# Attention scores of 64-row heads: one head on each half of TensorE's rows, instead of zero-padded queries on all 128 rows

## The chip, the core and the metric

The kernel runs on one core of one Trainium2 chip. The metric is the device time of one execution in microseconds (us). Matrix products run on TensorE (in the profile: PE for the matmul, PEld for the load of its stationary operand), elementwise work on VectorE (DVE), ScalarE (ACT) and GpSimd (POOL); transfers are issued from SyncE (SP). TensorE multiplies a stationary operand (up to 128 rows by 128 columns) with a moving one (the same rows, up to 512 columns) and adds into a bank of the accumulator memory (128 partitions by 512 fp32), of which there are eight.

## What is computed

Two layers of an encoder trunk on one sequence of 256 tokens, width 1024, in fp32. Each layer is a half-step feed-forward block, a mixer, a second half-step feed-forward block and a gated input embedding. The mixer's first half is neighbourhood attention with 8 heads of 64 channels, and only its scores are touched here:

```python
D_MODEL, SEQ, DEPTH, D_FF = 1024, 256, 2, 2816
NA_HEADS, NA_HEAD_DIM = 8, 64
...
    for i in range(DEPTH):
        x = x + 0.5 * swiglu(rmsnorm(x, g_ffa[i]), w_ffa_gate[i], w_ffa_up[i], w_ffa_down[i])
        u = rmsnorm(x, g_mix[i]) @ w_in[i]
        q, k, v, hy = jnp.split(u, [NA_WIDTH, 2 * NA_WIDTH, 3 * NA_WIDTH], axis=-1)
        y_na = neighbourhood_attention(q, k, v, na_rpb[i])   # scores, bias, mask, softmax, values
        ...                                                  # Hyena long convolution -> y_hy
        x = x + concat([_rms(y_na), _rms(y_hy)]) * g_out[i] @ w_out[i]
        x = x + 0.5 * swiglu(rmsnorm(x, g_ffb[i]), w_ffb_gate[i], w_ffb_up[i], w_ffb_down[i])
        x = x + jax.nn.sigmoid(rmsnorm(x, g_ple[i]) @ w_ple_gate[i]) * (p[i] @ w_ple_proj[i])
    return rmsnorm(x, g_final)
```

The kernel computes the scores of a head densely, all 256 queries against all 256 keys. Scaling, bias and mask (-1e30 outside the neighbourhood) come in one pass afterwards, and then the softmax.

## The kernel before

**Precision.** Every fp32 operand is split into a high part, rounded to the TensorE format fp32r, and a low part, the remainder. A product is the sum of three matmuls: high by high, high by low, low by high. `mm3` (L169) issues these three in a row and then counts them with `paced`; `Wide.mm` and `Wide.flush` (L190, L197) do the same for 512-wide operands that hold high and low parts side by side. Splitting is an ACT copy to fp32r and a DVE subtraction. The weights are split in this way while the kernel runs (L285 on ACT, L288 on DVE, or on POOL for every third piece of the mixer).

**Order of the work.** The order on PE is the order of the program text, and that on ACT is the order in which the program emits its instructions. Work beside the matmuls (evictions, splits, softmax) is written as fibers, generators that advance one step at each tick. `paced` counts matmul groups and calls a tick after every third count (`TICK = 3`); a fiber's `finish` forces ticks until that fiber is done. The mixer follows a written list (L58):

```python
ORDER = "g0 q0 g1 s0 q1 g2 t0 s1 g3 q2 t1 p0 u0 q3 f0 s2 f1 p1 s3 t2 x0 x1 t3 i0 p2 p3 i1 i2 i3 a0 ..."
```

Here `q` projects the queries and keys of one pair of heads, `s` makes the scores of a pair, `t` transposes its probabilities, `p` multiplies them with the values; `g`, `x`, `u`, `f` and `i` belong to the convolution and `a` to the output projection. There are four pairs in a layer, so eight in the run.

**Queries and keys.** A pair's projection leaves one bank: queries in columns 0 to 255, keys in columns 256 to 511; rows (partitions) 0 to 63 belong to the first head of the pair and 64 to 127 to the second. `QK.go` (L727 to L744) multiplies with the row norms on DVE (L733) into `q`. Then ACT copies the keys' high part (L738) and the queries' high part, 64 rows at a time (L740), and DVE makes the low parts (L742, L744). The queries go into tiles `qh` and `ql` of 128 by 512 that POOL has set to zero (L728, L729): head 0 lies in rows 0 to 63 of columns 0 to 255, head 1 in rows 64 to 127 of columns 256 to 511, and the rest stays zero.

**Scores.** `Head.scores` (L754 to L761) takes a bank, and for each half `tt` of the queries calls `mm3` with 128 zero-padded query columns as the stationary operand and all 256 key columns as the moving one. All 128 rows take part; the zeros remove the other head. That is 6 matmuls of 128 rows for a head and 12 for a pair, first all of head 0, then all of head 1. Each head's softmax fiber (L763 to L781: two DVE passes, two ACT exponentials, a reciprocal, two ACT scalings) is spawned right after that head's matmuls. `turn` (L783, transposes on L788) needs the finished softmax, and its result is split on L797 and L799. `attend` (L812) is the product with the values; `head_norm` (L804) scales its result on L807 and squares it on L353.

**What else uses these engines near the scores.** `spectral` (L895 to L914) has DVE products on L902 and L903, a POOL combination on L908 and a split on L912 (ACT) and L914 (DVE).

Of the kernel before, what the change touches and what calls it, by code (L numbers as in the profile page):

```python
# [12 lines left out]
F32R = mybir.dt.float32r  # L13
# [5 lines left out]
P = 128  # L19
T = 256  # L20
# [60 lines left out]
def hybrid_trunk(ctx: ExitStack, tc: tile.TileContext, w, xT, pT, rpb, small, wf, zT, dft, idft, decay, out):  # L81
    nc = tc.nc
    V, S, G, PE = nc.vector, nc.scalar, nc.gpsimd, nc.tensor
# [15 lines left out]
    def nm(s):  # L99
        uid[0] += 1  # L100
        return f"{s}{uid[0]}"

    def bank():
        return psp.tile([P, 512], F32, tag="ps", name=nm("ps"))

    def t2(dt=F32, s="t"):
        return k2.tile([P, 512], dt, tag="k2", name=nm(s))

    def t1(dt=F32, s="s"):
        return k1.tile([P, T], dt, tag="k1", name=nm(s))  # L110

    def v2(ap):
        return ap.rearrange("p (a b) -> p a b", a=2)

    def f(ap):
        return ap.bitcast(F32)
# [31 lines left out]
    def spawn(gen, first=False):  # L148
        fb = Fiber(gen)
        Pace.live.insert(0 if first else len(Pace.live), fb)  # L150
        return fb

    def tick():
        if not Pace.inside:
            Pace.inside = True
            for fb in list(Pace.live[::-1] if NEWEST else Pace.live):
                fb.step()
            Pace.live[:] = [fb for fb in Pace.live if not fb.done]
            Pace.inside = False
# [5 lines left out]
    def rest(n):  # L165
        for _ in range(n):
            yield

    def mm3(o, lh, ll, rh, rl, start, stop):  # L169
        PE.matmul(o, lh, rh, start=start, stop=False)  # L170
        PE.matmul(o, lh, rl, start=False, stop=False)  # L171
        PE.matmul(o, ll, rh, start=False, stop=stop)  # L172
        paced(o.free_size() // T if hasattr(o, "free_size") else o.shape[-1] // T)

    def paced(n=1):
        if not Pace.inside:
            Pace.total += 1
            Pace.count += n
            while Pace.count >= TICK:
                Pace.count -= TICK  # L180
                tick()
# [114 lines left out]
    def half():  # L296

        n = Stream.used
        Stream.used += 1
        h, l, fb = Stream.ready.pop(n)  # L300
        fb.finish()
        refill(n - LAG)
        return h, l
# [150 lines left out]
    def rb2():  # L454
        return rb.unsqueeze(1).to_broadcast([P, 2, T])
# [213 lines left out]
    def mixer(i):  # L669
# [15 lines left out]
        for quarter in range(4):  # L685
            h, l = half()
            for k in range(2):
                c = 2 * quarter + k
# [30 lines left out]
        class QK:  # L719


            def __init__(self, b):
                self.kh, self.kl = t1(F32R), t1(F32R)
                self.qh, self.ql = t2(F32R), t2(F32R)
                self.fb = spawn(self.go(b))

            def go(self, b):  # L727
                G.memset(f(self.qh), 0.0)  # L728
                G.memset(f(self.ql), 0.0)  # L729
                yield from rest(EV)  # L730
                yield from rs.wait()
                q = t2()
                V.tensor_tensor(v2(q), v2(b), rb2(), op=ALU.mult)  # L733
                yield
                where = [
                    (slice(64 * par, 64 * par + 64), slice(T * par, T * par + T)) for par in range(2)
                ]
                S.copy(self.kh, q[:, T:])  # L738
                for r, c in where:
                    S.copy(self.qh[r, c], q[r, :T])  # L740
                yield
                V.tensor_sub(self.kl, q[:, T:], f(self.kh))  # L742
                for r, c in where:
                    V.tensor_sub(self.ql[r, c], q[r, :T], f(self.qh[r, c]))  # L744

        class Head:

# [3 lines left out]
                self.bias = bp.tile([P, 2, T], F32, tag="bias", name=nm("bias"))  # L751
                nc.sync.dma_start(self.bias, rpb[i, 2 * pair + par])

            def scores(self, st):  # L754
                st.fb.finish()
                b = bank()
                for tt in range(2):
                    qs = slice(T * self.par + tt * P, T * self.par + (tt + 1) * P)
                    mm3(b[:, tt * T : (tt + 1) * T], st.qh[:, qs], st.ql[:, qs], st.kh, st.kl, True, True)
                self.e = t2()  # L760
                self.fb = spawn(self.softmax(b), True)  # L761

# [86 lines left out]
        def gated(c, b):  # L849
            t = t1(s="u")  # L850

            def go():
                res = [t1(), t1()]
                yield from conv(b, (8 + c, 4 + c), res)
                yield
                G.tensor_mul(t, *res)

            u.append((t, spawn(go())))
# [11 lines left out]

        def scores(pair, st):
            hs = [Head(pair, par) for par in range(2)]
            for h in hs:
                h.scores(st)
            return hs

        uT = []
# [1 line left out]
        def u_turned():  # L879
            for tt in range(2):  # L880
                b = bank()
                for c in range(4):
                    u[c][1].finish()
                    PE.transpose(b[:, c * P : (c + 1) * P], u[c][0][:, tt::2], ident)
                h, l = t2(F32R), t2(F32R)

                def go(b=b, h=h, l=l):
                    split(b, h, l)
                    yield

                uT.append((h, l, spawn(go())))
# [75 lines left out]
        qs, hs, added, wo = {}, {}, [], Tiles()  # L967
        for kind, j in MIXER:
            if kind == "g":
                gated(j, columns())  # L970
            elif kind == "q":
                qs[j] = QK(columns())
            elif kind == "x":
                outer(2 * j, columns())
            elif kind == "s":
                hs[j] = scores(j, qs.pop(j))
            elif kind == "t":
                turn(hs[j])
            elif kind == "p":
                attend(j, hs.pop(j))  # L980
                if len(yna) == 4:
                    na = Rstd(rna, nsq.parts, HY, [fb for _, fb in yna], STAT_NA, SPREAD_NA)
            elif kind == "u":
                u_turned()
            elif kind == "f":
                forward(j)
            elif kind == "i":
                backward(j)
                if len(yhy) == 4:
                    hy = Rstd(rhy, hsq.parts, HY, [fb for _, fb in yhy], STAT_HY, SPREAD_HY)  # L990
            elif kind == "a":
                added.append(spawn(add(j, project(wo, j, yna), na, G)))
# [126 lines left out]
    for j, ps in enumerate(outs):  # L1119
        tt, half_d = divmod(j, 2)  # L1120
        o = t2(s="o")
        r = fin.r[:, tt : tt + 1]
# [139 lines left out]
```

## Time and profile before

| | |
|---|---|
| median of 3 runs | 1102.88 us (1100.53 to 1103.08) |
| the profiled execution's own time | 1100.78 us |
| span of its instructions | 1099.0 us |
| mean granted TensorE clock | 0.994 of full speed |
| PEld busy | 964.8 us (88%) |
| DVE busy | 895.5 us (81%) |
| ACT busy | 645.6 us (59%) |
| POOL busy | 306.8 us (28%) |
| DMA | 194.06 MB, 177 GB/s |

Busy times of PE are modelled: a matmul's duration in the profile contains its way through the array, while the next one has already begun. So the distance from one start to the next, and not the duration, tells what a matmul costs in a dense row of them. In a line of the timeline the first number is the start in us from the span's beginning, the second the time that it (or the merged group) takes; `x4` counts merged instructions; square brackets hold the engine's idle time before it and what ended that. In a line of the groups, `x32 | 9.4, 294 | 0.9` means 32 instructions, 9.4 us busy in all, 294 ns each on average, and 0.9 us of idle time before them. A line of the stretches gives the window, its length, and for each engine the busy time and the number of instructions. Line numbers such as L170 are those of the kernel before.

### The profile page before, as it was taken

How to read it: one execution, taken by the hardware profiler on the slowest of the kernel's cores; microseconds unless marked ns; L12 is line 12 of the kernel's file. 1: busy time of each engine (PE TensorE's matmuls, PEld its weight loads, DVE VectorE, ACT ScalarE, POOL GpSimd, SP SyncE). 2: the span in 40 equal slices, each digit the busy share in tenths (PEclk: the TensorE clock that was granted, in tenths of full speed). 3: DMA queues.
4: the chain of work that ended last, by engine and by line, in shares of the span. 5: the costliest groups of instructions: out<-in, count | busy, mean ns of one | idle time of the engine just before them, and what ended most of it. 6: DMA issues, size and time to landing. Idle time of an engine off the chain costs nothing.

```text
span 1099.0 us, 17994 instructions
## 1 busy us (share of the span) xinstructions
PE 1069.0 (97%) x6716; PEld 964.8 (88%) x6716; DVE 895.5 (81%) x1552; ACT 645.6 (59%) x1182; POOL 306.8 (28%) x270
## 2 busy tenths in 40 slices
PE   7989999999998999999999999999999999999995
PEld 6878888899997888888988888889989888888895
DVE  4999987797999977766789989777899998776665
ACT  6566565377746755544656665544856575554444
POOL 3123231534363311111112113135442721111101
PEclk9999999999999999999999999999999999999998
DMA  8556554554425655555465654554522465555521
GB/s 318 196 201 230 194 189 155 185 185 154 148 78 201 199 189 190 189 192 191 155 208 185 233 192 166 186 185 152 194 77 95 147 207 215 191 193 181 185 94 38
DMA packets 32983, 194.06 MB, mean 177 GB/s; under 512 B 3584, under 2 KB 6528, under 8 KB 10880
## 3 DMA queue, kind: packets, MB, share of 16 engines
q1 hardware_dynamic: 32896, 192.92, 51.1%
q8 instruction: 52, 0.85, 0.3%
q14 instruction: 35, 0.29, 0.1%
HBM read 191.86 MB, written 1.05 MB: 176 GB/s over the span
## 4 chain that ended last, share of the span: by engine, by line
PE 80%; DVE 11%; ACT 4%; issue 3%; DMA 1%; POOL 0%; SPq 0%; DVEq 0%; ACTq 0%; POOLq 0%
PE ps L191 43%; PE ps L200 23%; PE ps L171 4%; PE ps L172 4%; PE ps L170 4%; DVE wl L288 2%; ACT wh L285 1%; DVE rt L399 1%; DVE s L841 1%; DVE x L945 1%; DVE s L944 1%; ACT t L781 1%; DMA t<-in_idft 1%; DVE xg L370 0%; DMA raw<-in_w 0%
## 5 line engine op out<-in xcount | busy, mean ns | idle before, releaser
L288 DVE TENSOR_TENSOR wl<-raw,wh 128x1024 fp32r<-128x1024 f32 (+1 forms) x328 | 416.3, 1272 | 135.1 <-ACT wh L285 113.3
L285 ACT CAST wh<-raw 128x1024 fp32r<-128x1024 f32 (+1 forms) x350 | 362.9, 1042 | 206.0 <-PE ps L191 143.5
L191 PE MATMUL ps<-xg,wh 128*128 128x512 f32 x1408 | 363.2, 396 | 12.3 <-DVE xg L1093 6.6
L191 PEld LDWEIGHTS ps<-xg,wh 128*128 128x128 f32 x1408 | 254.6, 191 | 59.4 <-DVE xg L370 7.5
L200 PEld LDWEIGHTS ps<-xg,wl 128*128 128x128 f32 x1408 | 195.4, 193 | 14.1
L200 PE MATMUL ps<-xg,wl 128*128 128x256 f32 x1408 | 200.5, 284 | 0.0
L490 POOL TENSOR_TENSOR gu<-gu,rb 128x256 f32<-128x256 f32 x88 | 94.8, 1082 | 368.1 <-DVE gu L208 288.0
L191 PE MATMUL ps<-act,wh 128*128 128x512 f32 x704 | 179.0, 392 | 0.0
L356 POOL TENSOR_TENSOR acc<-acc,q 128x256 f32<-128x256 f32 x62 | 68.9, 1112 | 283.7 <-ACT q L353 282.5
L191 PEld LDWEIGHTS ps<-act,wh 128*128 128x128 f32 x704 | 126.3, 189 | 22.1
L170 PE MATMUL ps<-xg,wh 128*128 128x256 f32 x448 | 127.5, 285 | 0.0
L172 PE MATMUL ps<-xg,wl 128*128 128x256 f32 x448 | 126.7, 283 | 0.0
L171 PE MATMUL ps<-xg,wh 128*128 128x256 f32 x448 | 126.7, 283 | 0.0
L200 PEld LDWEIGHTS ps<-act,wl 128*128 128x128 f32 x704 | 97.1, 190 | 7.6
L200 PE MATMUL ps<-act,wl 128*128 128x256 f32 x704 | 99.4, 282 | 0.0
L171 PEld LDWEIGHTS ps<-xg,wh 128*128 128x128 f32 x448 | 85.9, 192 | 0.1
L170 PEld LDWEIGHTS ps<-xg,wh 128*128 128x128 f32 x448 | 85.9, 192 | 0.1
L172 PEld LDWEIGHTS ps<-xg,wl 128*128 128x128 f32 x448 | 85.9, 192 | 0.0
L288 POOL TENSOR_TENSOR wl<-raw,wh 128x1024 fp32r<-128x1024 f32 x22 | 55.9, 2540 | 63.7 <-ACT wh L285 50.9
L208 DVE TENSOR_TENSOR gu<-gu,ps 128x256 f32<-128x256 f32 x176 | 71.9, 412 | 0.1
L205 ACT COPY gu<-ps 128x256 f32<-128x256 f32 x176 | 63.6, 369 | 0.0
L368 ACT ACTIVATE xg<-x,sm 128x256 fp32r<-128x256 f32 x56 | 28.1, 507 | 59.5 <-DVE x L529 40.2
(196 smaller groups left out, 1369.5 us busy)
## 6 DMA issues: line engine op xcount, KB each, us to landing
raw<-in_w SPq DMA_DIRECT2D x172, 1024.0 KB, 4.9
bias<-in_rpb SPq DMA_DIRECT2D x16, 256.0 KB, 2.8
raw<-in_w SPq DMA_DIRECT2D x4, 256.0 KB, 4.8
x<-in_xT SPq DMA_DIRECT2D x8, 128.0 KB, 4.7
raw<-in_w SPq DMA_DIRECT2D x2, 512.0 KB, 5.8
t<-in_wf SPq DMA_DIRECT2D x4, 256.0 KB, 5.4
dec<-in_decay SPq DMA_DIRECT2D x4, 256.0 KB, 5.4
out<-o SPq DMA_DIRECT2D x4, 256.0 KB, 2.4
```

Source lines behind the costliest of these rows:

```text
L170: PE.matmul(o, lh, rh, start=start, stop=False)
L171: PE.matmul(o, lh, rl, start=False, stop=False)
L172: PE.matmul(o, ll, rh, start=False, stop=stop)
L191: PE.matmul(b, lh, r, start=start, stop=False)
L200: PE.matmul(o, ll, rh, start=False, stop=stop)
L205: S.copy(dst, b[:, T:])
L208: V.tensor_add(dst, dst, b[:, :T])
L285: S.copy(h[:, a : a + k], src)
L288: e.tensor_sub(l[:, a : a + k], src, f(h[:, a : a + k]))
L356: G.tensor_add(self.ac, self.ac, q)
L368: S.activation(hl[:, :T], x[c], AF.Copy, scale=g)
L490: G.tensor_mul(u, u, rb)
```

## The change

The score matmuls take 64 rows instead of 128. The stationary operand is rows 0 to 63 (head 0) or 64 to 127 (head 1) of 128 query columns, and the moving one the same rows of the 256 key columns. The two heads alternate matmul by matmul, each into its own bank. The number of score matmuls stays at 12 for a pair. Queries and keys are split together, by one ACT copy and one DVE subtraction of 128 by 512, in place of three of each; the zero-padded tiles, their memsets on POOL and the separate key tiles go away. Both heads' softmax fibers are spawned after all 12 matmuls. `paced` is called after each pair of matmuls, six times for a pair of heads; before, `mm3` called it four times.

```diff
             def __init__(self, b):
-                self.kh, self.kl = t1(F32R), t1(F32R)
-                self.qh, self.ql = t2(F32R), t2(F32R)
+                self.h, self.l = t2(F32R), t2(F32R)
                 self.fb = spawn(self.go(b))
 
             def go(self, b):
-                G.memset(f(self.qh), 0.0)
-                G.memset(f(self.ql), 0.0)
                 yield from rest(EV)
                 yield from rs.wait()
                 q = t2()
                 V.tensor_tensor(v2(q), v2(b), rb2(), op=ALU.mult)
                 yield
-                where = [
-                    (slice(64 * par, 64 * par + 64), slice(T * par, T * par + T)) for par in range(2)
-                ]
-                S.copy(self.kh, q[:, T:])
-                for r, c in where:
-                    S.copy(self.qh[r, c], q[r, :T])
-                yield
-                V.tensor_sub(self.kl, q[:, T:], f(self.kh))
-                for r, c in where:
-                    V.tensor_sub(self.ql[r, c], q[r, :T], f(self.qh[r, c]))
+                S.copy(self.h, q)
+                yield
+                V.tensor_sub(self.l, q, f(self.h))
 
         class Head:
...
-            def scores(self, st):
-                st.fb.finish()
-                b = bank()
-                for tt in range(2):
-                    qs = slice(T * self.par + tt * P, T * self.par + (tt + 1) * P)
-                    mm3(b[:, tt * T : (tt + 1) * T], st.qh[:, qs], st.ql[:, qs], st.kh, st.kl, True, True)
+            def scored(self, b):
                 self.e = t2()
                 self.fb = spawn(self.softmax(b), True)
...
         def scores(pair, st):
             hs = [Head(pair, par) for par in range(2)]
-            for h in hs:
-                h.scores(st)
+            st.fb.finish()
+            banks = [bank(), bank()]
+            for tt in range(2):
+                qs = slice(tt * P, (tt + 1) * P)
+                for n, (a, b) in enumerate(((st.h, st.h), (st.h, st.l), (st.l, st.h))):
+                    for par, o in enumerate(banks):
+                        r = slice(64 * par, 64 * par + 64)
+                        PE.matmul(o[:, tt * T : (tt + 1) * T], a[r, qs], b[r, T:], start=n == 0, stop=n == 2)
+                    paced()
+            for h, o in zip(hs, banks):
+                h.scored(o)
             return hs
```

## The prediction

> **What bounds the kernel now.** I read the page's busy times first, then its chain.
>
> ```profile
> span 1099.0 us, 17994 instructions
> PE 1069.0 (97%) x6716; PEld 964.8 (88%) x6716; DVE 895.5 (81%) x1552; ACT 645.6 (59%) x1182; POOL 306.8 (28%) x270
> PE 80%; DVE 11%; ACT 4%; issue 3%; DMA 1%; POOL 0%; SPq 0%; DVEq 0%; ACTq 0%; POOLq 0%
> ```
>
> PE is busy for 97% of the span and makes 80% of the chain. Where PE runs without a gap, a matmul less moves everything behind it forward. Where PE waits for DVE or ACT, a matmul less only makes it wait longer. So for every group of scores the question is which kind of stretch follows it. First the scores themselves, in the groups by line and shape, and inside pair 0 of layer 0 in the timeline:
>
> ```profile
> L170 PE MATMUL ps<-s,t 128*128 128x256 f32 x32 | 9.4, 294 | 0.9 <-ACT t L740 0.9
> L170 PEld LDWEIGHTS ps<-s,t 128*128 128x128 f32 x32 | 6.1, 190 | 1.3 <-ACT t L740 1.3
> ```
>
> ```profile
> 237.38 0.28 PE L170 MATMUL ps<-s,t 128*128 128x256 f32 x1
> 237.39 0.19 PEld L171 LDWEIGHTS ps<-s,t 128*128 128x128 f32 x1
> 237.50 0.28 PE L171 MATMUL ps<-s,t 128*128 128x256 f32 x1
> ...
> 238.34 0.28 PE L172 MATMUL ps<-s,t 128*128 128x256 f32 x1
> 238.46 0.28 PE L170 MATMUL ps<-xg,wh 128*128 128x256 f32 x1
> ```
>
> `mm3` has three lines, L170 to L172, with 32 matmuls each: 96, or 12 for each of 8 pairs. The modelled duration is 0.28 us, but from 237.38 to 238.46 nine matmuls start, so one costs 1.08 / 9 = 0.12 us, and the load of the next (237.39) lies under the running one (237.38). All scores take 96 x 0.12 = 11.5 us, 1% of the span; nothing that this change does can be worth much more than half of that on PE.
>
> **What the change takes from PE.** If the two heads' matmuls run side by side on the two halves of the rows, a pair of matmuls costs what one costs now. That is 48 x 0.12 = 5.8 us, or 0.72 us for each pair of heads. If they run one after the other, it is nothing. No row shows a 64-row matmul, so these are the two ends. I take the first as likelier: no row shows two matmuls that share an array part, and the two heads share no rows and, by the diff, no bank. What speaks against it is the stationary operand's load, since each half still needs one of its own:
>
> ```profile
> 305.66 0.50 PE L418 MATMUL ps<-onesf,nacc 128*128 128x1 f32 x4
> 306.02 0.36 PE L170 MATMUL ps<-idft_h,t 128*128 128x256 f32 x1
> 306.23 0.28 PE L171 MATMUL ps<-idft_l,t 128*128 128x256 f32 x1
> ```
>
> Four matmuls of a single moving column take 0.36 us, 0.09 each, although they have nothing to stream: that is about the cost of a load of 128 columns. If loads of the two halves can't overlap each other, a pair costs at least 2 x 0.09 = 0.18 us, and 48 x (0.24 - 0.18) = 2.9 us is the most that is won.
>
> The row of 237.39 bears on a second doubt: a load starts 0.01 us after the matmul before it, on the same rows. The Trainium skill ("TensorE: Matmul & The Clock Gate", the mechanism under Part 3 on packing small matmuls) says that a load overlaps a running matmul only where its row group differs. By that rule each half would load and stream in turn, and a pair would cost about what two matmuls cost now, so nothing would be won; the trace disagrees with it for full rows, and shows nothing for halves.
>
> **Changing over between 128 and 64 rows** happens twice for each pair, 16 times. The nearest rows for a change of kind are those at 306.02 and 306.23: after the single-column matmuls the distance is 0.21 us where 0.12 is usual, 0.09 more. The upper bound is a whole refill: the time by which a matmul's duration exceeds its distance, 0.28 - 0.12 = 0.16 us, and a load that isn't hidden, 0.09: 0.25 us. The lower bound is nothing; a gain from it has no ground. I take 0.09, the nearest row.
>
> **Where the saved time goes, pair by pair.** Pair 0 of layer 0 starts with a wait:
>
> ```profile
> 234.63 0.68 DVE L733 TENSOR_TENSOR t<-ps,rb 128x512 f32<-128x512 f32 x1
> 235.23 1.21 DVE L288 TENSOR_TENSOR wl<-raw,wh 128x1024 fp32r<-128x1024 f32 x1
> 235.35 0.41 ACT L738 CAST s<-t 128x256 fp32r<-128x256 f32 x1 [3.45 <-DVE t L733]
> 236.11 0.39 PE L170 MATMUL ps<-s,t 128*128 128x256 f32 x1 [0.62 <-ACT t L740]
> 236.83 0.38 PE L171 MATMUL ps<-s,t 128*128 128x256 f32 x1 [0.34 <-DVE s L742]
> 237.16 0.38 PE L172 MATMUL ps<-s,t 128*128 128x256 f32 x1
> ```
>
> ```profile
> L738 ACT CAST s<-t 128x256 fp32r<-128x256 f32 x8 | 3.3, 408 | 13.1 <-DVE t L733 13.1
> L740 ACT CAST t<-t 64x256 fp32r<-64x256 f32 x16 | 6.4, 403 | 0.2
> L742 DVE TENSOR_TENSOR s<-t,s 128x256 fp32r<-128x256 f32 x8 | 5.8, 726 | 0.5 <-ACT s L738 0.5
> L744 DVE TENSOR_TENSOR t<-t,t 64x256 fp32r<-64x256 f32 x16 | 6.7, 418 | 0.2
> L912 ACT CAST t<-t 128x512 fp32r<-128x512 f32 x8 | 4.7, 615 | 0.0
> L914 DVE TENSOR_TENSOR t<-t,t 128x512 fp32r<-128x512 f32 x8 | 5.3, 683 | 0.0
> ```
>
> ```profile
> 807.54 2.62 DVE L742 TENSOR_TENSOR s<-t,s 128x256 fp32r<-128x256 f32 x1
> ```
>
> The new split has the shapes of L912 and L914. For each pair ACT does 0.62 us in place of 0.41 + 2 x 0.40 = 1.21, and DVE 0.68 in place of about 0.42 + 2 x 0.42 = 1.26 (the mean of L742, 0.73, holds the one of 2.62; an undisturbed one, at 812.19 below, takes 0.42). DVE finishes L733 at 235.31, so the high part is there at about 235.35 + 0.62 = 235.97. The low part needs DVE, which L288 holds until 236.44: 236.44 + 0.68 = 237.12, against 237.16 for the same point now. Ten of twelve matmuls then remain in both versions. Ten half-row matmuls take 0.6 us in place of 1.2. So pair 0 gains 0.6 us, and behind it lie the projections q1 and g2, on which PE is dense. Pair 1 lies between t0 and g3 without a wait of its own, and gains the whole 0.72. For two layers: 2 x (0.6 + 0.72) = 2.6 us.
>
> Pairs 2 and 3 are different. The transposes t2 come straight after the scores s3, and need the softmax of pair 2:
>
> ```profile
> 812.19 0.42 DVE L742 TENSOR_TENSOR s<-t,s 128x256 fp32r<-128x256 f32 x1
> 812.52 0.87 DVE L744 TENSOR_TENSOR t<-t,t 64x256 fp32r<-64x256 f32 x2
> 813.43 0.69 DVE L903 TENSOR_TENSOR t<-ps,spec 128x512 f32<-128x512 f32 x1
> 814.04 1.28 DVE L767 SCALAR_TENSOR_TENSOR t<-ps,bias 128x512 f32<-128x512 f32 x2
> ```
>
> ```profile
> 815.94 0.51 ACT L774 ACTIVATE t<-t,mx 128x256 f32<-128x256 f32 x1 [3.09 <-DVE mx L769]
> ...
> 818.55 1.87 ACT L781 ACTIVATE t<-t,ri 128x256 f32<-128x256 f32 x4
> ```
>
> ```profile
> 817.63 0.28 PE L172 MATMUL ps<-s,t 128*128 128x256 f32 x1
> 819.11 1.91 PE L788 MATMUL ps<-ident,t 128*128 128x128 f32 x8 [1.20 <-ACT t L781]
> ```
>
> ```profile
> 807.00:821.00 14.00, 12.64 (x80) 10.84 (x79) 13.88 (x24) 6.27 (x20) 7.11 (x6) 1.00 0.23 75
> 272.00:285.00 13.00, 12.87 (x83) 11.35 (x83) 11.36 (x22) 6.78 (x20) 7.32 (x6) 1.00 0.35 122
> ```
>
> In layer 1, DVE (the third busy time) is full: 13.88 of 14 us. PE would go on at 817.63 + 0.12 = 817.75 and waits until 819.11, 1.36 us, at the end of a chain that starts with L767 on DVE. What PE saves in s2 and s3 is worth nothing there. What DVE saves is: the splits of pairs 2 and 3 lie ahead of L767, each 1.26 - 0.68 = 0.58 us shorter, so t2 can start about 1.2 us earlier, which is still no earlier than PE can be there (1.36 + 1.44 us of slack). Layer 0 has slack on DVE (11.36 of 13), and its transposes follow L781 with a chain in which p1's result stands:
>
> ```profile
> 281.89 0.48 ACT L807 ACTIVATE y<-ps,sm 128x256 fp32r<-128x256 f32 x1 [0.56 <-PE ps L172]
> 282.53 1.70 ACT L781 ACTIVATE t<-t,ri 128x256 f32<-128x256 f32 x4
> ```
>
> ACT waits 0.56 us for p1's matmuls, which come after s2 and before s3. So s2's 0.72 us moves t2 forward, up to what the exponentials allow (those gain the 0.58 of DVE), and s3's 0.72 turns into waiting. I take 0.65. Behind t2, PE is dense again (x0, x1).
>
> **The sum.** 2.6 (pairs 0 and 1) + 1.2 (layer 1) + 0.65 (layer 0) = 4.45 us. Of the 16 changes-over, those ahead of a wait cost nothing: both ends of s2 and s3 in layer 1, both ends of s3 in layer 0 and the entries of s0, eight in all. Eight remain: 8 x 0.09 = 0.7 us; with 0.25 each, 2 us. Net: -3.7 us, between -4.5 and -2.4. The memsets go from POOL, which has nothing late for want of them. The banks are asked for together, and there are eight in rotation. `paced` counts six instead of four for a pair: eight counts more in a layer, some 2.7 ticks, and a new phase for everything behind. A tick is three groups of three matmuls, about 1.1 us, so each later wait of PE on DVE or ACT may move by part of that; I add 1.5 us to both sides for it and nothing to the middle. Against the profiled execution (1100.78 us, of which 1.8 lie around the span) the sum gives 1097.1. The median is 2.1 us above that execution, so against 1102.88 it gives 1099.2.
>
> **Rivals.**
>
> *The halves run one after the other* (loads in turn, or a half's load that waits for its own matmul). Then PE saves between nothing and 2.9 us, DVE's 1.2 us at t2 of layer 1 remain, and the changes-over cost 0.7 to 2 us. Head 0's softmax now starts only behind all twelve matmuls; DVE's order (L767 at 814.04, long after s2) covers that. Near -1: 1101.9 us. For it: the 0.09 us of a load; against it: that the halves share no rows. Chance 0.30.
>
> *The changes-over drain the array.* Side by side, but at least 0.25 us for each exposed change, and perhaps twice that with the load of both halves: -4.45 + 2 to 4, near -1.5: 1101.4 us. For it: the 0.28 us duration, which an emptied array has to wait out; against it: the change of kind at 306.02 costs only 0.09. The Trainium skill ("TensorEngine Tiling (Array Packing)", Key Properties) says that changing the tiling mode drains the engine; no run here shows it yet. Chance 0.16.
>
> *Slower: the load is no longer hidden.* If a load for one half can't run under any matmul, as it does at 237.39, each of the 96 matmuls pays its 0.09 us on top of 0.12: +8.6, with the changes-over +0.7 to +2, less 1.2 at t2: near +8.5, 1111.4 us. It decides from 0.04 us of exposed load for each matmul (96 x 0.04 - 1.2 + 0.7 = 3.3). Against it: full rows hide it everywhere. Chance 0.14.
>
> **How the numbers follow.** My forecast has the remaining chance, 0.40, at 1099.2 us, with its own range 1096.9 to 1102.0. About 0.3% (3.3 us) is what a measurement can tell from no change. Faster by more: 0.26 of the forecast's 0.40 (its middle lies 0.4 us beyond that line), 0.04 of the drain and 0.05 of the serial case, where loads overlap in part: 0.35. Slower by more: 0.12 of the unhidden load, 0.03 of the serial case with dear changes-over: 0.15. Same: 0.50. The range reaches from the forecast's lower end, 1096.9, past the serial case with 2 us of changes-over and 1.5 us of phase (1102.88 - 1.2 + 2 + 1.5 = 1105.2) to 1105.5, and leaves out most of the unhidden load.
>
> **What would show it.** Score matmuls of 64 rows whose starts come in twos, with 0.12 us from two to two and some 0.72 us for a group: the forecast. A steady 0.09 to 0.12 us from one to the next: serial. A first distance above 0.25 us on entering and leaving: the drain. 0.2 us between all: the unhidden load. At t2 of layer 1 the transposes should start about 1.2 us earlier after s2's end, and DVE should have 0.58 us less to do for each pair. The forecast is wrong if the score groups shorten and the kernel doesn't, which would mean that later waits have taken it back.

## The result and the profile after

The changed kernel takes 1106.63 us (median of 7 runs, 1105.36 to 1107.32), against 1102.72 for the kernel before in 7 runs. The ratio is 1.0052, with a 95% interval of 1.0041 to 1.0063: slower by 0.5%, where I had forecast 1099.2 us and a range that ended at 1105.5 us. (The two medians alone give 1.0035; a repeat, e9 below, gives 1.0054.) The profiled execution's own time is 1106.63 us too.

The page of the changed kernel:

```profile
span 1104.9 us, 17917 instructions
PE 1068.6 (97%) x6716; PEld 962.8 (87%) x6716; DVE 894.6 (81%) x1536; ACT 642.3 (58%) x1166; POOL 298.0 (27%) x254
```

ACT and POOL have less work, as planned, but DVE has hardly less (894.6 us against 895.5). The groups by line and shape say why (L732 to L734 are the new split, L865 the score matmuls):

```profile
L734 DVE TENSOR_TENSOR t<-t,t 128x512 fp32r<-128x512 f32 x8 | 9.9, 1237 | 1.4 <-ACT t L732 1.4
L732 ACT CAST t<-t 128x512 fp32r<-128x512 f32 x8 | 5.0, 623 | 16.0 <-DVE t L730 16.0
```

The low-part subtraction takes 1.24 us on average, where the prediction put 0.68. Now the place of the largest wait, t2 of layer 1. The timeline of PE:

```profile
818.77 0.39 PE L865 MATMUL ps<-t 64*128 64x256 f32 x2
818.99 0.40 PE L865 MATMUL ps<-t,t 64*128 64x256 f32 x4
819.23 0.28 PE L865 MATMUL ps<-t 64*128 64x256 f32 x2
819.35 0.40 PE L865 MATMUL ps<-t,t 64*128 64x256 f32 x4
822.97 2.10 PE L773 MATMUL ps<-ident,t 128*128 128x128 f32 x8 [3.22 <-ACT t L766]
```

The half-row matmuls do run side by side: they start in twos, and from 818.99 to 819.23 two pairs pass, 0.12 us for each pair. Then PE is idle for 3.22 us, where the kernel before had 1.20. In layer 0 the wait is 3.22 us as well, where the kernel before came to t2 without one (283.09, right behind the scores). The chain behind it, on DVE, POOL and ACT (L752 is the softmax's first pass, L896 and L897 the spectral products, L906 the split behind them, L766 the softmax's scaling):

```profile
810.20 2.89 DVE L734 TENSOR_TENSOR t<-t,t 128x512 fp32r<-128x512 f32 x1
813.02 0.68 DVE L730 TENSOR_TENSOR t<-ps,rb 128x512 f32<-128x512 f32 x1
814.38 0.69 DVE L734 TENSOR_TENSOR t<-t,t 128x512 fp32r<-128x512 f32 x1 [0.69 <-ACT t L732]
814.99 0.68 DVE L896 TENSOR_TENSOR t<-ps,spec 128x512 f32<-128x512 f32 x1
...
816.79 0.68 DVE L897 TENSOR_TENSOR t<-ps,spec 128x512 f32<-128x512 f32 x1
817.38 1.28 DVE L752 SCALAR_TENSOR_TENSOR t<-ps,bias 128x512 f32<-128x512 f32 x2
```

```profile
809.27 3.28 POOL L288 TENSOR_TENSOR wl<-raw,wh 128x1024 fp32r<-128x1024 f32 x1 [5.16 <-ACT wh L285]
```

```profile
821.63 0.36 ACT L353 ACTIVATE q<-ps 128x256 f32<-128x256 f32 x1
821.89 0.61 ACT L906 CAST t<-t 128x512 fp32r<-128x512 f32 x1
822.40 1.71 ACT L766 ACTIVATE t<-t,ri 128x256 f32<-128x256 f32 x4
```

Three things are new. From 814.99 on, four spectral products stand ahead of the softmax, 2.4 us; before, L767 came right behind the second of them, and the third and fourth followed the softmax's two passes. On ACT, the split L906 now stands ahead of the scaling L766. And at 810.20 the subtraction of pair 2 takes 2.89 us beside a POOL subtraction; in layer 0 it takes 2.89 us as well (at 271.73). There the kernel before lost 2.2 us in layer 1 (807.54) and nothing in layer 0 (0.41 us at 269.94).

The wait has a second price. The stretches around t2, for the changed kernel and the kernel before (the number behind the engines is the granted clock):

```profile
819.60:827.30 7.70, 4.41 (x24) 3.77 (x21) 6.87 (x14) 7.18 (x21) 3.65 (x3) 0.78 0.00 0
824.70:827.20 2.50, 2.50 (x14) 2.50 (x12) 2.50 (x5) 2.10 (x5) 1.02 (x1) 0.51 0.00 0
```

```profile
818.00:821.00 3.00, 1.73 (x10) 1.11 (x11) 3.00 (x7) 2.94 (x9) 3.00 (x4) 1.00 0.01 3
```

In the changed kernel the granted clock is 0.78 on average of the stretch, and 0.51 from 824.7 to 827.2, behind the idle time; in the kernel before it stayed at 1.00, from 820.7 to 832.4 too.

### The profile page after: what moved, and what is told of

Read it like the earlier page. It is cut to its first block, busy times and chain, and to the rows that moved or that the text cites. A ratio compares the mean times of both kernels' runs of the same rounds, so it can differ in the third digit from the quotient of the medians.

```text
span 1104.9 us, 17917 instructions
## 1 busy us (share of the span) xinstructions
PE 1068.6 (97%) x6716; PEld 962.8 (87%) x6716; DVE 894.6 (81%) x1536; ACT 642.3 (58%) x1166; POOL 298.0 (27%) x254
## 5 line engine op out<-in xcount | busy, mean ns | idle before, releaser
L191 PE MATMUL ps<-xg,wh 128*128 128x512 f32 x1408 | 363.5, 397 | 12.6 <-DVE xg L1087 6.5
L191 PEld LDWEIGHTS ps<-xg,wh 128*128 128x128 f32 x1408 | 255.1, 191 | 60.0 <-DVE xg L370 8.1
L191 PE MATMUL ps<-act,wh 128*128 128x512 f32 x704 | 179.1, 392 | 0.0
L191 PEld LDWEIGHTS ps<-act,wh 128*128 128x128 f32 x704 | 126.1, 189 | 22.0
L356 POOL TENSOR_TENSOR acc<-acc,q 128x256 f32<-128x256 f32 x62 | 64.3, 1038 | 286.0 <-ACT q L353 284.8
L288 POOL TENSOR_TENSOR wl<-raw,wh 128x1024 fp32r<-128x1024 f32 x22 | 59.0, 2680 | 71.8 <-ACT wh L285 71.8
```

The lines of the kernel that those rows point to most:

```text
L191: PE.matmul(b, lh, r, start=start, stop=False)
L288: e.tensor_sub(l[:, a : a + k], src, f(h[:, a : a + k]))
L356: G.tensor_add(self.ac, self.ac, q)
```

## The experiments

I tell three theories apart. **O (order):** the two additional `paced` counts for each pair of heads change the order on DVE and ACT, so that the softmax of pair 2 comes late. **R (rows):** half-row matmuls and the changes between 128 and 64 rows cost the time. **C (collision):** the larger subtraction is held up beside POOL. All runs have the kernel before on the same chip.

| run | edit | us | ratio to before (95%) |
|---|---|---|---|
| e9 | the changed kernel again | 1106.18 | 1.0054 (1.0038 to 1.0070) |
| e1 | four counts | 1099.03 | 0.9990 (0.9981 to 1.0000) |
| e2 | t2 behind x0 | 1106.82 | 1.0054 (1.0040 to 1.0068) |
| e3 | before, t2 behind x0 | 1103.07 | 1.0016 (1.0004 to 1.0027) |
| e4 | full rows, changed order, six counts | 1110.49 | 1.0094 (1.0079 to 1.0109) |
| e5 | one head after the other | 1108.25 (one run) | |
| e6 | softmax a tick earlier, six counts | 1100.98 | 1.0008 (1.0000 to 1.0017) |
| e7 | e4 with four counts | 1100.29 | 1.0004 (0.9992 to 1.0015) |
| e8 | e1, s2 ahead of f0 | 1100.59 | 1.0011 (1.0001 to 1.0021) |
| e10 | e1 and e6 together | 1099.81 | 0.9996 (0.9983 to 1.0008) |
| e11 | before, six counts | 1111.19 | 1.0095 (1.0079 to 1.0111) |
| e12 | e1, other third on POOL | 1093.00 | 0.9936 (0.9919 to 0.9952) |
| e13 | before, other third on POOL | 1097.46 | 0.9973 (0.9961 to 0.9985) |
| e14 | changed, other third on POOL | 1103.50 | 1.0031 (1.0020 to 1.0042) |
| e15 | e1, last third on POOL | 1104.83 | 1.0043 (1.0028 to 1.0058) |

### The counts: e1, e4, e7, e11, e6

e1 takes the two additional counts out of the changed kernel:

```diff
-                    paced()
+                    if n:
+                        paced()
```

> The changed kernel, with paced called four times for a pair of heads, as before the change, in place of six. Theory O (order): the two extra counts moved two products of the convolution's spectral step ahead of the softmax on DVE; without them the softmax of pair 2 begins about 1.2 us earlier in each layer, the wait at the transposes t2 falls from 3.2 us to 2 us or less, so that the clock is no longer halved behind it: 1102 to 1103 us. Theory R (rows): the half-row matmuls and the changes between 64 and 128 rows cost the time: still 1106 us. Theory C (collision): the larger subtraction of pair 2, held up beside a POOL subtraction (2.89 us in place of 0.68), costs the time: still near 1106 us.

It takes 1099.03 us, less than O expected. No matmul and no split differs from the changed kernel, so the two counts cost 0.64% there (1.0054 / 0.9990), about 7 us, more than the whole loss. DVE again has two spectral products ahead of the softmax (L897 and L898 are these products here):

```profile
808.55 0.68 DVE L897 TENSOR_TENSOR t<-ps,spec 128x512 f32<-128x512 f32 x1
809.15 0.68 DVE L898 TENSOR_TENSOR t<-ps,spec 128x512 f32<-128x512 f32 x1
809.74 1.28 DVE L752 SCALAR_TENSOR_TENSOR t<-ps,bias 128x512 f32<-128x512 f32 x2
```

e4 keeps the 128-row matmuls, splits and memsets and takes the changed order alone: heads alternate, both softmaxes are spawned at the end, six counts.

```diff
+                for n, (a, b) in enumerate(((st.qh, st.kh), (st.qh, st.kl), (st.ql, st.kh))):
+                    for par, o in enumerate(banks):
+                        qs = slice(T * par + tt * P, T * par + (tt + 1) * P)
+                        PE.matmul(o[:, tt * T : (tt + 1) * T], a[:, qs], b, start=n == 0, stop=n == 2)
+                    paced()
```

> The kernel before with its 128-row zero-padded matmuls, splits and memsets, but in the changed order: heads alternate into two banks, both softmaxes are spawned at the end, six counts. Theory O: the order alone makes the wait at t2 longer: 1105 to 1107 us. Theories R and C: no half rows and no larger subtraction, so like the kernel before, 1102.7 us.

1110.49 us: more than O expected, and R and C, which expected no loss, fail. e7 puts `if n:` ahead of that `paced()`:

> The kernel e4 (128-row matmuls, heads alternating, both softmaxes spawned at the end) with four counts. Theory O: the counts alone made e4 slow, so this is within 2 us of the kernel before. Against e1, which differs from it in the half rows and the splits: e1 should lie 3 us below it if the saving on TensorE reaches the end, and not below it if DVE sets the pace there.

1100.29 us, a ratio of 1.0004: alternating heads and late softmaxes cost nothing by themselves. Against it e1 lies 0.1% lower, with intervals that overlap; so with four counts the saving on TensorE hardly shows in the whole time (the table below tells where it went). e11 does the reverse and puts the two counts alone into the kernel before:

```diff
             for h in hs:
                 h.scores(st)
+                paced()
```

> The kernel before, whole, with one extra paced call after each head's scores: six counts in place of four for a pair, and nothing else. Theory O: the counts alone cost most of the loss; on DVE the softmax of head 0 has two spectral products ahead and that of head 1 has four: 1104 to 1108 us, although no matmul has changed. Theory R: equal to the kernel before.

1111.19 us, above the expected range, with not one instruction added. On DVE (L903 and L904 are the spectral products here, L767 the first softmax pass of either head) and PE:

```profile
821.05 0.68 DVE L767 SCALAR_TENSOR_TENSOR t<-ps,bias 128x512 f32<-128x512 f32 x1
821.65 0.68 DVE L903 TENSOR_TENSOR t<-ps,spec 128x512 f32<-128x512 f32 x1
822.25 0.68 DVE L769 TENSOR_REDUCE mx<-t 128x2 f32<-128x512 f32 x1
822.84 0.68 DVE L904 TENSOR_TENSOR t<-ps,spec 128x512 f32<-128x512 f32 x1
823.43 0.68 DVE L767 SCALAR_TENSOR_TENSOR t<-ps,bias 128x512 f32<-128x512 f32 x1
```

```profile
827.10 0.94 PE L788 MATMUL ps<-ident,t 128*128 128x128 f32 x4 [2.17 <-ACT t L781]
```

The first pass of head 1 (823.43) now stands behind four products; that of head 0 still has two ahead of it. e6 leaves the six counts and removes the softmax fiber's first rest:

```diff
                 e = self.e
-                yield from rest(EV)
```

> The changed kernel with its six counts, but the softmax fibers start a tick earlier (their first rest is left out). Theory O1 (the place of the softmax behind four spectral products on DVE costs the time): only two products lie ahead again, so 1100 us or less, like e1. Theory O2 (the phase of the ticks changes something else, further on): it stays near 1106 us.

1100.98 us, 1 us above what O1 expected, but with all six counts in place 0.46% come back (1.0054 to 1.0008), some 5 us. On DVE only two products stand ahead of the softmax again (L895, L896 and L751 here), and still the subtraction of pair 2 takes 2.89 us:

```profile
805.05 2.89 DVE L734 TENSOR_TENSOR t<-t,t 128x512 fp32r<-128x512 f32 x1
...
810.43 0.68 DVE L896 TENSOR_TENSOR t<-ps,spec 128x512 f32<-128x512 f32 x1
811.03 1.28 DVE L751 SCALAR_TENSOR_TENSOR t<-ps,bias 128x512 f32<-128x512 f32 x2
```

So most of the loss is the softmax's place behind the spectral products, O1. A part of the 0.18% that e6 still lies above e1 is a second effect of the counts: in layer 0, e6 has the subtraction of pair 2 beside POOL's (2.89 us at 269.13), like the changed kernel, and e1 has not (0.69 us at 266.58). e10 joins both remedies:

> The kernel e1 (half rows, four counts) with the softmax started a tick earlier, as in e6. If the number of ticks between the scores and t2 set the wait, the two remedies add: 2 us below e1. If the order on DVE sets it (the list of DVE is the same as in e1 up to the softmax: two spectral products ahead of it), nothing is added: within 1.5 us of e1.

1099.81 us, no different from e1: one place in the order, mended twice.

Where in the mixer the time goes can be read from the starts of the same matmuls in two traces: the first of g0, of s3, of t2, of t3 and of the next feed-forward block (L191); in layer 0 of the changed kernel these are 216.72, 280.29, 284.49, 298.58 and 334.71. The differences, both layers together, in us (each trace is one execution; the repeat e9 differs from the changed kernel by at most 0.2 in any column):

| | g0 to s3 | s3 to t2 | t2 to t3 | t3 to the next block | sum before rounding |
|---|---|---|---|---|---|
| changed less e1 (two counts, half rows) | +1.4 | +4.5 | +0.8 | +0.6 | +7.4 |
| e11 less before (two counts, full rows) | +2.8 | +3.3 | +2.3 | +2.1 | +10.5 |
| e6 less changed (softmax earlier) | -1.4 | -3.4 | -2.3 | +1.8 | -5.4 |
| e1 less e7 (half rows, four counts) | -2.2 | -0.4 | +1.4 | 0.0 | -1.3 |
| e12 less e13 (changed rows against before, other third) | -2.9 | -0.4 | 0.0 | -0.6 | -3.9 |

The wait at t2 and the stretch behind it hold 5.3 of the 7.4 us in the changed kernel and 5.6 of the 10.5 us in e11. In layer 0 the two effects can be told apart there: from s3 to t2 the changed kernel takes 2.8 us longer than e1, of which 1.7 us go with the softmax's place (e6) and 1.1 us stay in e6 with the subtraction held up. The rest of what the counts cost lies ahead of s3 and behind t3; no run takes it apart. The fourth row shows that TensorE's saving is real: by t2 e1 is 1.2 us ahead of e7 in layer 0 and 1.4 us in layer 1. In layer 1 it is all lost behind t2, where e1's granted clock falls after 1.50 us of idle time (below) and e7's stays at 1.00 after 1.18 us.

### Moving t2 or s2: e2, e3, e8

```diff
-... f1 p1 s3 t2 x0 x1 t3 ...
+... f1 p1 s3 x0 t2 x1 t3 ...
```

> The changed kernel, with the transposes t2 one place later, behind the projection x0 (5.8 us of matmuls). Theories O and C: the loss is a wait at t2, which x0 now covers, and the halved clock behind it: 2 x (3.2 + 1.4) us less, 1097 to 1098 us. Theory R: only the wait that the kernel before had as well goes away, some 2 us: 1104 us.

> The kernel before, with t2 behind x0: the control for the run e2. Its waits at t2 (0.6 us in layer 0, about 2.2 us in layer 1) go away: 1100 us by all theories. With the wait covered on both sides, O and C expect e2 below this run by 8 x 0.4 = 3 us, R expects e2 above it by 3 us or more.

Both expectations failed: 1106.82 and 1103.07 us, nothing gained by the changed kernel and 0.16% lost by the one before. The wait at t2 went (no idle time there in the trace of e2), but came back at t3 and in the matmuls after it:

```profile
832.57 1.75 PE L773 MATMUL ps<-ident,t 128*128 128x128 f32 x8 [0.57 <-ACT t L766]
836.21 0.39 PE L170 MATMUL ps<-idft_h,t 128*128 128x256 f32 x1 [0.83 <-ACT t L906]
838.08 0.39 PE L172 MATMUL ps<-idft_h,t 128*128 128x256 f32 x1 [1.36 <-DVE t L908]
```

So covering this one wait is no remedy here: the next consumers of ACT's and DVE's results wait. e8 puts the scores ahead of the transform instead (`q3 s2 f0 f1`, from e1):

> The kernel e1 (half rows, four counts) with the scores s2 placed before the transform f0 in place of behind it, so that the softmax of pair 2 starts some 2.8 us sooner and ahead of the spectral products on DVE. If what is left of the loss in e1 is the wait for that softmax at t2 and the halved clock behind it, 1.5 to 3 us per layer go: 1095 us. If DVE as a whole bounds the stretch from u0 to t3, the wait only moves to t3 and the time stays within 1.5 us of e1.

1100.59 us: no gain, and 0.21% above e1 (1.0011 / 0.9990), 2.3 us, so even the bound of the second case was missed by a little. The wait has moved, though not to t3 but to the scores themselves:

```profile
808.03 0.50 PE L865 MATMUL ps<-t,t 64*128 64x256 f32 x4 [2.01 <-DVE t L734]
```

It is the low part of pair 2, whose subtraction takes 2.84 us there, beside POOL. That pointed to C as a second loss.

### The collision: e12 to e15

In the mixer every third weight piece is subtracted on POOL. e12 takes another third, in the kernel e1:

```diff
-                e = G if Stream.on_pool and n % Stream.on_pool == 0 else V
+                e = G if Stream.on_pool and n % Stream.on_pool == 1 else V
```

> The kernel e1 with another third of the mixer's weight pieces on POOL (every third piece counted from one in place of from zero), so that the POOL subtraction no longer meets the low-part subtraction of pair 2, which takes 2.88 us beside it in place of 0.68. Theory C: that collision is what is left at t2 and t3: 2 x 1 to 2 us below e1. If DVE's work as a whole bounds the stretch, another DVE instruction is held up in its place: within 1.5 us of e1.

1093.00 us, the best of all versions and below both kernels; more than C expected. In its trace DVE is no longer held up at pair 2, and t2 of layer 1 waits 0.44 us:

```profile
802.18 0.68 DVE L734 TENSOR_TENSOR t<-t,t 128x512 fp32r<-128x512 f32 x1
```

```profile
812.16 1.92 PE L773 MATMUL ps<-ident,t 128*128 128x128 f32 x8 [0.44 <-ACT t L766]
```

But POOL's work has moved rather than gone: now the subtraction of pair 0 is held up in both layers, and s0 of layer 0 waits 1.47 us for it.

```profile
233.61 2.27 DVE L734 TENSOR_TENSOR t<-t,t 128x512 fp32r<-128x512 f32 x1 [0.69 <-ACT t L732]
```

The same edit in the kernel before and in the changed kernel:

> The kernel before with the other third of the mixer's weight pieces on POOL, as in e12: the control for e12. If e12's gain is that of the half rows, set free from the collision, the kernel before gains only what its own collision in layer 1 cost (2.62 us in place of 0.42), 1 to 2 us: 1099 us, and e12 lies 5 us or more below it. If the other third is simply the better one for any version, the kernel before gains the same 7 us: 1093.5 us.

> The changed kernel (six counts) with the other third on POOL. If counts and collision are two separate losses, it gains some 6 us from e9, to 1100 us, and stays some 7 us above e12. If the counts cost only because DVE was held up by the collision, it comes within 2 us of e12: 1093 to 1095 us.

e13 takes 1097.46 us, between its two expectations: the other third as such is worth 0.27% to the kernel before. Against it e12 is 0.37% lower (0.9936 / 0.9973), about 4.1 us; taking the two intervals end against end, 0.66% to 0.09%. That is what half rows, their splits and the changed order are worth with this third, with pair 0 held up in both kernels alike (2.23 us at 235.18 in e13). e14 takes 1103.50 us, 0.96% above e12 (1.0031 / 0.9936), although POOL holds up the same subtractions in both, those of pair 0: with this third the two counts cost as much as in e11. So the counts are a loss of their own. But the two losses do not simply add up, as the expectation had it: with six counts the other third is worth 0.23% (1.0054 to 1.0031), 2.5 us in place of some 6. e15 takes the remaining third (`== 2`):

> The kernel e1 with the remaining third of the weight pieces on POOL (every third, counted from two). If it is the meeting with the scores' splits of pair 2 that matters, this third is free of it as well and gains 4 to 7 us against e1: 1093 to 1095 us. If e12 won by chance of order elsewhere, it stays near 1099 us or above.

It missed: 1104.83 us. Pair 2 is mostly free of the collision there too (0.69 us in layer 0, 1.69 in layer 1), but the start of the next feed-forward block waits longer:

```profile
337.32 3.78 PE L191 MATMUL ps<-xg,wh 128*128 128x512 f32 x8 [4.64 <-DVE xg L370]
```

In each layer this costs 3.7 us more than in e1 between t3 and that block. So the choice of the third acts on several places, and e12's 0.54% against e1 (0.9936 / 0.9990) can't be put down to the one collision alone. The traces show the collision's share: from s3 to t3 of layer 1, where e1's pair 2 is held up, e12 gains 2.4 us on e1 and e15 2.6 us, 1.1 us of it at t2 and the rest behind it; in layer 0, where e1's is not, neither gains anything there.

### Do the halves run side by side? e5

```diff
-                for n, (a, b) in enumerate(...):
-                    for par, o in enumerate(banks):
+            for par, o in enumerate(banks):
+                for tt in range(2): ...
```

> The changed kernel, with all six matmuls of head 0 (rows 0 to 63) before the six of head 1 (rows 64 to 127) in place of alternating; six counts as in the changed kernel. If the gain on TensorE comes from the two halves running side by side, the starts within a head are 0.12 us apart and a group takes some 1.4 us plus the changes-over, against 0.9 to 1.1 us in the changed kernel. If 64-row matmuls are quicker in themselves, the group stays at about 1 us.

Neither number came out. The group s1 in the trace:

```profile
250.62 0.38 PE L865 MATMUL ps<-t 64*128 64x256 f32 x1
250.84 0.40 PE L865 MATMUL ps<-t,t 64*128 64x256 f32 x2
250.97 0.39 PE L865 MATMUL ps<-t 64*128 64x256 f32 x2
251.19 0.40 PE L865 MATMUL ps<-t,t 64*128 64x256 f32 x4
251.43 0.28 PE L865 MATMUL ps<-t 64*128 64x256 f32 x1
251.55 0.40 PE L865 MATMUL ps<-t,t 64*128 64x256 f32 x2
251.88 0.39 PE L170 MATMUL ps<-xg,wh 128*128 128x256 f32 x1
252.10 0.28 PE L171 MATMUL ps<-xg,wh 128*128 128x256 f32 x1
```

Twelve matmuls take 1.26 us, between the 0.9 to 1.1 of alternating halves and the 1.4 of one after the other. The starts are single at first and at the end and come mostly in twos in the middle: nine distinct starts for twelve matmuls, the three twos within 0.01 us (at 250.97, 251.20 and 251.32). Three must have run beside others, although the program has the two heads one after the other. So the time of a group does hang on how many stand side by side, and alternating is worth 0.36 us against this order.

## Why the prediction was wrong

**TensorE's saving: right in kind.** The forecast side by side, 0.12 us for two, is what 818.99 and 819.23 show; loads in turn and unhidden loads are out. **The changes-over: too low.** Taken at 0.09 us each. In the rows of e5, where 0.12 is usual, the second score matmul comes 0.22 us after the first (250.62 to 250.84); on leaving, 0.21 lie between the last score (251.55 and one step of 0.12) and 251.88, and 0.22 more to 252.10. On entering pair 3 of the same run, 0.21 us lie ahead of the first score (280.77 to 280.98). The changed kernel's own rows agree on entering: 0.22 us from 818.77 to 818.99. So each change costs 0.09 on one side and 0.10 on the other, 0.19 us in all, between my 0.09 and my upper bound of 0.25, and a group keeps about 0.72 - 2 x 0.19 = 0.34 us. This is a smaller drain than the rival had at its low end, and not what decided the sign.

**DVE's saving: right for the shapes, lost to the counts.** The step "DVE 0.68 in place of about 1.26" took the undisturbed duration for all eight. Measured in the changed kernel: 9.9 us for the eight against 5.8 + 6.7 = 12.5 for L742 and L744, so 0.3 us for each pair in place of 0.58. But e1 makes the same subtractions in 7.7 us, 0.6 us less for each pair than before, and e11, which has the old shapes, takes 7.7 us for L742 in place of 5.8 (e1 is the first line, e11 the second):

```profile
L734 DVE TENSOR_TENSOR t<-t,t 128x512 fp32r<-128x512 f32 x8 | 7.7, 963 | 2.9 <-ACT t L732 2.9
L742 DVE TENSOR_TENSOR s<-t,s 128x256 fp32r<-128x256 f32 x8 | 7.7, 966 | 0.0
```

With six counts pair 2 meets POOL's subtraction in both layers, with four only in layer 1, whichever the shape (e4 and e7 agree: 7.7 and 5.8 us for L742). So theory C was wrong to blame the larger subtraction; the place decides, and the counts moved it. I had seen the 2.62 us of L742 and set it aside as one instance. The Trainium skill ("SBUF — State Buffer", Who interferes with whom) says that a DVE instruction with two SBUF inputs contends with a GpSimd instruction that reads SBUF; the 2.89 us at 810.20, beside the POOL row of 809.27, agree.

**The step that failed:** "`paced` counts six instead of four for a pair ... a new phase for everything behind ... I add 1.5 us to both sides for it and nothing to the middle." The two counts cost 0.64% to 0.96% in four comparisons (e9 against e1, e4 against e7, e11 against the kernel before, e14 against e12), 7 to 10.5 us. They do not just shift later waits a little in both directions; they put the softmax of pair 2 behind two more spectral products (in the full-row kernel e11, that of head 1), and the subtraction of pair 2 in layer 0 beside POOL's. For layer 1 the prediction had quoted the rows that told the first: L767 follows L903 directly at 814.04, and DVE is busy for 13.88 of 14 us. It asked how much DVE work was saved there, but not what order DVE would have. Layer 0 had slack on DVE (11.36 of 13 us), and the wait at t2 grew there the most, from none to 3.22 us; so the slack that it had before did not protect it.

**"Behind t2, PE is dense again"** missed a third thing: behind this long wait the granted clock is lower (0.51 from 824.7 to 827.2). From 824.72 (x0) to 837.39 (t3) the changed kernel takes 12.67 us, the kernel before 11.59 for the same matmuls (820.78 to 832.37):

```profile
824.72 0.56 PE L170 MATMUL ps<-xg,wh 128*128 128x256 f32 x1
...
837.39 1.03 PE L773 MATMUL ps<-ident,t 128*128 128x128 f32 x8
```

```profile
820.78 0.36 PE L170 MATMUL ps<-xg,wh 128*128 128x256 f32 x1
...
832.37 1.03 PE L788 MATMUL ps<-ident,t 128*128 128x128 f32 x8
```

**The sum.** Net -3.7 us was forecast. With the order mended (e1) only 0.1% came, and with the other third on both sides (e12 against e13) 0.37%, 4.1 us. So the forecast came near the change's own worth with that third (the intervals allow 1.0 to 7.3 us), and the kernel that was built spent more than that on two counts. That the sum fits so well is partly luck: by t2, e12 is 2.1 us ahead of e13 in layer 0 and 1.3 us in layer 1, where the terms of the sum had 1.5 and 2.2 us. The prediction's last sign came true: the score groups shortened, the kernel did not, and later waits took it back. Shown: the cost of the counts, by four pairs of kernels; the softmax's place as its largest part in the changed kernel, by e6 and the traces. Not settled: what the counts cost ahead of s3 and behind t3, and why the choice of POOL's third acts on the start of the next block.

## What to carry to other kernels

Where a program's order on an engine follows from counted ticks, a change in what is counted is a change of schedule: compare the order on each engine around the tightest stretch before forecasting, and keep the count as it was when a unit of work becomes smaller. Look at what stands ahead of the step that others wait for, even on an engine with some slack; moving the consumer away (e2, e8) only moved the wait here. A duration far above its group's others hints at a collision: ask which other instructions will meet under the new order, and don't drop it as an outlier.

## What the runs showed of the hardware that I had not expected

- Matmuls of 64 rows on the other half of the array started ahead of program order (e5: three of twelve).
- The same idle time does not always cost the clock. In e1 and in e6, t2 of layer 1 starts after 1.50 us of idle time by the profile. In e1 the stretch behind it was granted 0.67, in e6 1.00. What tells them apart is open:

```profile
814.80:820.00 5.20, 5.09 (x26) 4.42 (x27) 5.20 (x11) 5.14 (x13) 3.11 (x3) 0.67 0.01 2
```

```profile
816.10:821.00 4.90, 4.76 (x36) 4.29 (x37) 4.90 (x9) 4.90 (x13) 3.12 (x3) 1.00 0.00 0
```
